# First FFN's weight sums on VectorE, and the output product's first blocks in the memory of a later step's sums

## The chip, the cores and the metric

The kernel is one program on one core of a Trainium2 chip. The core has five engines that run their own instruction streams in order: TensorE (PE in the profile, with PEld for its weight loads), VectorE (DVE), ScalarE (ACT), GpSimd (POOL) and SyncE (SP), which here does nothing but issue transfers. Work on one engine waits for another engine or for a transfer by semaphores. Tiles lie in SBUF; the products are accumulated in PSUM banks. Time is device time of one execution, in microseconds (us); the figure for a kernel is the median of its runs, and lower is better.

## What is computed

One layer of a decoder with 16 meta tokens in front of 1024 tokens, width 1024, all in float32:

```python
h = h + 0.5 * swiglu(rms_norm(h, ffn1_norm), ffn1_w_in, ffn1_w_out)   # first FFN
u = rms_norm(h, mix_norm) @ w_in
o = concat(hgrn2(u...), stick_breaking(u...))                         # the mixer
h = h + o @ w_out
h = h + 0.5 * swiglu(rms_norm(h, ffn2_norm), ffn2_w_in, ffn2_w_out)   # second FFN

def swiglu(h, w_in, w_out):
    g, u = split(h @ w_in, 2)          # w_in: 1024 x 5632, so g and u are 2816 wide
    return (silu(g) * u) @ w_out       # w_out: 2816 x 1024
```

The change lies in the two FFNs, in the first above all. An FFN has an *input product* (h @ w_in, then the gate silu(g) * u) and an *output product* (the gated activations @ w_out).

## The kernel before, in words

**Products.** A float32 product is made as three matmuls on a rounded type: each operand is split into a high half (a cast on ScalarE) and a low half (the operand minus its high half, on VectorE), and TensorE multiplies high by high, low by high and high by low. Both products of an FFN save an eighth of the multiplications with a scheme of Strassen and Winograd: operands are cut into 2 x 2 blocks, and seven products of sums of blocks stand for eight products of blocks.

**The input product** is `fast_in` (L351). It goes through the 2816 columns of g and u in eleven pairs of blocks of 128; of each pair of blocks it does first the gate's part and then the up part. Such a part is a *quad* (L450). A quad takes the four 128x512 blocks of w_in that belong to 256 columns and both halves of the depth: a11, a21, a22, a12. `block` (L368) has SP load each into a tile `raw`; there are `in_bufs` of them in turn (10 in the first FFN). Four sums are made of them, by `made` (L377; the instruction is L382, its tile is `s`): s1 = a21 + a22, s2 = s1 - a11, s3 = a11 - a21, s4 = a12 - s2. In this kernel they are made on GpSimd. `operand` splits a block or a sum into `wh` (ScalarE, L361) and `wl` (VectorE, L363). `times` (L441; its matmuls are L445) multiplies it in twelve matmuls of 512 columns by one of the seven operands of activations. The order of the seven products on TensorE, with the bank of PSUM each adds to, is

```
B11 (a11, qa)  T2 (s2, qb)  B21 (a12, qa)  T3 (s3, qb)  T1 (s1, qc)  T4 (a22, qb)  B22 (s4, qc)
```

Where two products go to one bank, the second adds to what the first left. Before that, partial sums that other outputs need are read out: `first` (L464) copies p1 from qa, and `kept` (L472; VectorE, L477) makes u2 = p1 + qb ahead of T3's product and u3 = p1 + qb after it. Then `take` hands each finished output on: for a gate quad to `gate` (VectorE L523, ScalarE's silu), for an up quad to `up` (VectorE L533 and L534), which multiplies by the gate. The up quad's outputs are four tiles `sg`; three are stored at once (L537). Of all four, `combined` (L543) makes the operands T1 to T4 of the output product by four subtractions on VectorE (L552 twice, L559, L562) and stores them through GpSimd's queue. In the first FFN `combined` is *put off*: it is appended to `put_off` and called in the next gate quad, behind the call that makes u3.

**Side work in the first FFN.** Meant to fill idle time of other engines, it is dealt out over the input product by hooks (`taken`, L1777): parts of other weights are read, split and stored to DRAM for later (`split_ahead`, L142; L152 loads, L179 and L180 split into a tile `both`, L174 stores it as `w2in` or `wout`), and x is turned (`turn_x`, L984). The meta tokens' input product (`meta_in`, L932) is made in small matmuls in the up quad; for it the gate's and the up's raw blocks are both held.

**The opening.** The first four pairs of quads of the first FFN (two in the second) are *opened*: they run interleaved while their activation operands are still made. In the first FFN `open_tokens` (L765) writes out the order by hand, as items 2 to 15. At item 4 it calls `prepare(0)` (L406), which loads the four blocks of the first quad and makes their four sums.

**The output product** is `fast_out` (L606). It goes through seven steps, each over eleven blocks q of 256 rows of w_out:

```
A12  A11  S1  S2  S4  S3  A22
```

`left(step, q)` (L644) gives the block or sum of w_out: S1 = A21 + A22, S2 = S1 - A11, S4 = A12 - S2, S3 = A11 - A21. Blocks that are needed once come into the ring of tiles `raw` (7 in the first FFN, 6 in the second); two tiles stay for the whole product: `sk`, eleven blocks that S1 fills first and S2 and S3 overwrite, and `ak`, eleven blocks of A11. `right` loads the activations, `halved` (L634) splits both into the tile `parts`, which has four places for weights, and the matmuls are L707. The meta tokens' output product (`meta`, L1875; `meta_block`, its matmuls are L1865) uses the raw blocks of A12, S3 and A22 and so holds them: in A12 it runs after every third q.

**What sets the order.** TensorE's order is written by hand. The other engines' orders come from a planner that goes by estimated costs and times at which operands are ready, except in the opening, where ScalarE's, VectorE's and SP's are by hand too. `self.tc.issue_after(x)` asks for no wait: it only puts what is issued under it behind x in the order of the same engine. `self.apart` is true in the first FFN's output product alone. The pools for the output product are laid over memory that the input product has used, and waits between old and new tiles are put in by the framework (`reuse_waits="tile"`, L49).

## Time and profile before

| | |
|---|---|
| median of 3 runs | 2025.84 us (2024.75 to 2028.49) |
| the profiled execution | 2025.31 us, its span 2023.6 us |
| mean granted clock of TensorE | 0.998 |
| first FFN, input product / output product | about 16 to 493 us / 493 to 722 us |
| second FFN, input product / output product | about 1376 to 1801 us / 1801 to 2014 us |

How to read the rows. A group of instructions is named by its line, its engine and its tiles, out<-in by the names in the program, with partitions x elements and how many there were; then the busy time in us with the mean of one in ns, and behind a second bar the idle time of the engine just before these instructions and what ended it ("<-DVE u L477": VectorE's instruction on `u` at line 477). A wait is read as "who waits, on which tile and line <- for whom: us in all, how many times, the longest". A time line's row has the start, the duration, the engine and the instruction. TensorE's clock is the clock that was granted, as a share of full speed.

### The profile page before, as it was taken

Reading aid. Unit: us, or ns where it says so; the run is one execution under the profiler, and the core shown is the slowest. Engines: PE = TensorE matmul, PEld = TensorE weight load, DVE = VectorE, ACT = ScalarE, POOL = GpSimd, SP = SyncE. Lnnn points to the kernel's source line nnn. Section 1 sums busy time; section 2 is a strip of 40 time slices with the busy share of each in tenths; the row PEclk is TensorE's granted clock in tenths of the full one; section 3 lists DMA queues with packets and bytes.
Section 4 is the critical chain, followed back from the end, with each engine's and each line's share of the span. In section 5 each row is a group of like instructions: output and inputs, shape, how many; then the busy total and the mean of one; then the engine's idle time right before and its main releaser. Section 6 shows DMA issues by size and latency. Waiting matters only on the chain.

```text
span 2023.6 us, 30784 instructions
## 1 busy us (share of the span) xinstructions
PE 1964.1 (97%) x10940; PEld 1647.1 (81%) x10940; DVE 1365.5 (67%) x2052; ACT 861.0 (43%) x1731; POOL 584.2 (29%) x692
## 2 busy tenths in 40 slices
PE   7999999999999999999999999999999999999998
PEld 6788787777778888897988888787888888888887
DVE  7877677787587663337777668548466776767774
ACT  6423343334344444356666644434132333244443
POOL 4344333332000002334333341320445544530000
PEclk9999999999999999999999999999999999999999
DMA  7257787656995406443545156674633332369463
GB/s 210 80 149 207 216 266 221 219 203 252 322 302 154 147 33 206 133 167 100 152 121 144 57 209 194 162 249 152 202 104 100 109 104 94 107 244 312 125 200 135
DMA packets 315577, 347.17 MB, mean 172 GB/s; under 512 B 61520, under 2 KB 216656, under 8 KB 315424
## 3 DMA queue, kind: packets, MB, share of 16 engines
q1 hardware_dynamic: 297136, 292.18, 46.5%
q0 software_dynamic: 17248, 53.03, 7.6%
q8 instruction: 86, 1.41, 0.3%
q14 instruction: 67, 0.55, 0.1%
q10 hardware_dynamic: 1040, 0.00, 0.0%
HBM read 233.75 MB, written 111.38 MB: 171 GB/s over the span
## 4 chain that ended last, share of the span: by engine, by line
PE 76%; DVE 4%; DMA 3%; issue 2%; ACT 1%; POOL 0%; SPq 0%; DVEq 0%; POOLq 0%; ACTq 0%
PE o L707 18%; PE qb L445 13%; PE qc L445 9%; PE qa L445 8%; PE proj L250 5%; PE proj L252 5%; PE proj L251 5%; PE flip L1398 2%; DMA raw<-in_ffn_w_out_dram 1%; PE wo L250 1%; PE wo L251 1%; PE wo L252 1%; PE lvl L1191 1%; PE oacc L1468 1%; PE oacc L1470 1%
## 5 line engine op out<-in xcount | busy, mean ns | idle before, releaser
L445 PE MATMUL qb<-T,wh 128*128 128x512 f32 x1056 | 348.2, 394 | 13.8 <-DVE u L477 11.8
L445 PEld LDWEIGHTS qb<-T,wh 128*128 128x128 f32 x1056 | 199.6, 189 | 62.9 <-issue 12.3
L445 PE MATMUL qa<-B,wh 128*128 128x512 f32 x696 | 227.5, 391 | 2.0 <-ACT both L469 1.7
L363 DVE TENSOR_TENSOR wl<-s,wh 128x512 fp32r<-128x512 f32 x160 | 184.2, 1151 | 57.1 <-ACT wh L361 55.8
L707 PE MATMUL o<-t,w 128*128 128x512 f32 x924 | 214.5, 391 | 4.1 <-DVE w L639 2.1
L250 PE MATMUL proj<-xh,wh 128*128 128x512 f32 (+2 forms) x640 | 216.5, 338 | 0.8 <-DVE st L1091 0.7
L252 PE MATMUL proj<-xl,wh 128*128 128x512 f32 (+2 forms) x640 | 209.7, 328 | 0.8 <-DVE xl L1853 0.8
L707 PE MATMUL o<-parts 128*128 128x512 f32 x924 | 209.9, 389 | 0.0
L251 PE MATMUL proj<-xh,wl 128*128 128x512 f32 (+2 forms) x640 | 209.8, 328 | 0.0
L445 PE MATMUL qb<-T,wl 128*128 128x512 f32 x528 | 206.9, 392 | 1.2 <-DVE wl L363 1.2
L707 PEld LDWEIGHTS o<-t,w 128*128 128x128 f32 x924 | 172.3, 188 | 43.6 <-DVE w L639 4.1
L707 PEld LDWEIGHTS o<-parts 128*128 128x128 f32 x924 | 173.4, 188 | 35.9
L361 ACT CAST wh<-s 128x512 fp32r<-128x512 f32 x160 | 99.4, 622 | 224.7 <-PE qb L445 181.0
L445 PEld LDWEIGHTS qa<-B,wh 128*128 128x128 f32 x696 | 130.5, 188 | 30.8 <-ACT both L469 1.9
L382 POOL TENSOR_TENSOR s<-raw 128x512 f32<-128x512 f32 x80 | 112.2, 1403 | 142.7 <-DMA raw<-in_ffn_w_in_dram 84.3
L361 ACT CAST wh<-raw 128x512 fp32r<-128x512 f32 x120 | 74.5, 622 | 148.1 <-PE qc L445 100.8
L445 PE MATMUL qa<-B,wl 128*128 128x512 f32 x348 | 135.5, 389 | 0.0
L252 PEld LDWEIGHTS proj<-xl,wh 128*128 128x128 f32 x640 | 120.5, 188 | 12.2 <-DVE xl L1853 1.2
L250 PEld LDWEIGHTS proj<-xh,wh 128*128 128x128 f32 x640 | 120.7, 189 | 11.4 <-DVE st L1091 1.2
L251 PEld LDWEIGHTS proj<-xh,wl 128*128 128x128 f32 x640 | 120.6, 188 | 9.1
L1550 POOL TENSOR_TENSOR sig<-sig,keep 128x144 f32<-128x144 f32 (+3 forms) x64 | 81.4, 1273 | 133.9 <-DVE keep L1544 79.9
L445 PEld LDWEIGHTS qb<-T,wl 128*128 128x128 f32 x528 | 99.9, 189 | 21.7 <-DVE wl L363 1.6
(392 smaller groups left out, 4042.5 us busy)
## 6 DMA issues: line engine op xcount, KB each, us to landing
raw<-in_ffn_w_in_dram SPq DMA_DIRECT2D x176, 256.0 KB, 4.0
raw<-in_ffn_w_out_dram SPq DMA_DIRECT2D x121, 256.0 KB, 4.5
w2in<-both SPq DMA_DIRECT2D x28, 512.0 KB, 3.2
raw<-in_w_in_dram SPq DMA_DIRECT2D x25, 512.0 KB, 4.1
ks<-kD SPq DMA_DIRECT2D x32, 260.0 KB, 4.7
wout<-both SPq DMA_DIRECT2D x16, 512.0 KB, 3.3
wh<-w2in SPq DMA_DIRECT2D x27, 256.0 KB, 3.3
wl<-w2in SPq DMA_DIRECT2D x27, 256.0 KB, 3.1
```

Source lines behind the costliest of these rows:

```text
L250: nc.tensor.matmul(ps, wh[:, s], xs, start=k == 0, stop=False)
L251: nc.tensor.matmul(ps, wl[:, s], xs, start=False, stop=False)
L252: nc.tensor.matmul(ps, wh[:, s], xl[:, k, c0 : c0 + n], start=False, stop=k == nk - 1)
L361: nc.scalar.copy(hi, src)
L363: nc.vector.tensor_sub(lo, src, hi.bitcast(F32))
L382: taken(op(t, x, y), False)
L445: nc.tensor.matmul(ps, a[:, k, :], b[:, k, :], start=start and k == 0 and i == 0, stop=k == 3 and i == 2, skip_group_check=True,)
L707: nc.tensor.matmul(banks[bank][m], y[:, m * P : (m + 1) * P], z, start=start and at == 0 and e == 0, stop=q == nq - 1 and e == 2, skip_gro ...
L1191: nc.tensor.matmul(ps[:, :, c, :], kp[:, P * c : P * c + P], strided(QA, P * c + n, (512 - n, 2), (2 * n, nb), (1, n)), start=True, stop=True,
L1398: self.nc.tensor.transpose(ps[:m, j, :], src[:, s0 : s0 + m], self.ident)
L1468: nc.tensor.matmul(o[:, c], vj, w[0], start=j == 0, stop=False, skip_group_check=True)
L1550: nc.gpsimd.tensor_mul(sig, sig, keep[:, 1 : nk + 1])
```

## The change

It has five parts.

1. In the first FFN the sums s1 to s4 of a quad are made on VectorE (`on`); those of `prepare(0)` stay on GpSimd, and so do the second FFN's.
2. `kept` remembers its last instruction, and the put-off `combined` is issued behind it: its four subtractions come behind u3 in VectorE's order.
3. In both FFNs the output product's first step, A12, loads its blocks into `sk[:, q]` and not into the ring. In the first FFN the meta tokens' matmuls for A12 are all made at the step's last q.
4. In the first FFN's output product what `left` issues on VectorE comes, in VectorE's order, behind the low half of the weights of four blocks before (`los[-4]`).
5. `prepare(0)` is called at item 11 of the opening and no longer at item 4.

```diff
--- before.py
+++ after.py
@@ -363,7 +363,7 @@
             nc.vector.tensor_sub(lo, src, hi.bitcast(F32))
             return hi, lo
 
-        loaded, put_off = [], []
+        loaded, put_off, last_kept = [], [], []
 
         def block(i, h, col):
             t = wp.tile([P, 4, P], F32, tag="raw", name="raw", bufs=self.in_bufs)
@@ -398,15 +398,17 @@
         prepared = {}
         quarters = (0, 0), (1, 0), (1, 1), (0, 1)
 
-        def first_sums(blocks, turns):
+        on = nc.vector if meta else nc.gpsimd
+
+        def first_sums(blocks, turns, on):
             a11, a21, a22, _ = blocks
-            s1 = made(a21, nc.gpsimd.tensor_add, a22, turns)
-            return s1, made(s1, nc.gpsimd.tensor_sub, a11, turns)
+            s1 = made(a21, on.tensor_add, a22, turns)
+            return s1, made(s1, on.tensor_sub, a11, turns)
 
         def prepare(col):
             blocks = [block(i, h, col) for i, h in quarters]
             a11, a21, _, a12 = blocks
-            s1, s2 = first_sums(blocks, 2)
+            s1, s2 = first_sums(blocks, 2, nc.gpsimd)
             s3 = made(a11, nc.gpsimd.tensor_sub, a21, 2)
             prepared[col] = blocks, (s1, s2, s3, made(a12, nc.gpsimd.tensor_sub, s2, 2))
 
@@ -427,16 +429,16 @@
             if sums:
                 s1, s2, s3, s4 = sums
             else:
-                s1, s2 = first_sums(blocks, turns)
+                s1, s2 = first_sums(blocks, turns, on)
             yield operand(s2)
             if not opened:
                 yield operand(a12)
-            yield operand(s3 if sums else made(a11, nc.gpsimd.tensor_sub, a21, turns))
+            yield operand(s3 if sums else made(a11, on.tensor_sub, a21, turns))
             if meta:
                 meta(col, [(q, b) for q, b in zip(quarters, blocks)])
             yield operand(s1)
             yield operand(a22)
-            yield operand(s4 if sums else made(a12, nc.gpsimd.tensor_sub, s2, turns))
+            yield operand(s4 if sums else made(a12, on.tensor_sub, s2, turns))
 
         def times(ps, w, x, start):
             (wh, wl), (xh, xl) = w, x
@@ -474,7 +476,9 @@
                     t = wp.tile([P, n], F32, tag="s", name=name, bufs=3)
                 else:
                     t = ev["p"].tile([P, n], F32, tag=name, name=name, bufs=1 if feed else 2)
-                taken(nc.vector.tensor_add(t, y, x), False)
+                last_kept[:] = [nc.vector.tensor_add(t, y, x)]
+                taken(last_kept[0], False)
+                last_kept[0] = last_kept[0].ins
                 return t
 
             if opened:
@@ -496,7 +500,8 @@
                 take(0, 0, go("a", "B21", False), None)
             u3 = kept("u3", p1, go("b", "T3", False))
             if put_off:
-                put_off.pop()()
+                with self.tc.issue_after(last_kept[0]):
+                    put_off.pop()()
             yield
             take(1, 1, go("c", "T1", True), u3)
             yield
@@ -636,10 +641,12 @@
             turns[name] = (i + 2) % 8
             hi, lo = (self.parts[name][:, j, :m] for j in (i, i + 1))
             nc.scalar.copy(hi, src)
-            nc.vector.tensor_sub(lo, src, hi.bitcast(F32))
+            at = nc.vector.tensor_sub(lo, src, hi.bitcast(F32))
+            if name == "w":
+                los.append(at.ins)
             return hi, lo
 
-        sub = nc.vector.tensor_sub
+        sub, los = nc.vector.tensor_sub, []
 
         def left(step, q):
 
@@ -665,9 +672,11 @@
                     return u, {(0, 0): a, (1, 0): s}
                 sub(a, a, raw(1, 0, q))
                 return a, {}
-            at = (0, 1) if step == "A12" else (1, 1)
-            t = raw(*at, q)
-            return t, {at: t}
+            if step == "A12":
+                nc.sync.dma_start(s, block(0, 1, q))
+                return s, {(0, 1): s}
+            t = raw(1, 1, q)
+            return t, {(1, 1): t}
 
         banks = {}
         delayed, opening = [], []
@@ -693,7 +702,8 @@
                     pout.tile([P, n], F32, tag=f"{bank}{m}", name="o") for m in range(4)
                 ]
             for q in range(nq):
-                src, blocks = left(a, q)
+                with self.tc.issue_after(los[-4]) if self.apart and len(los) > 4 else ExitStack():
+                    src, blocks = left(a, q)
                 act = right((q, b), n)
                 with self.tc.high_priority() if self.apart and a == "A12" and q < 3 else ExitStack():
                     wh, wl = halved(src, "w", 512)
@@ -892,13 +902,14 @@
         items = {
             2: lambda: (spare(2, 3), sums(1)),
             3: lambda: (spare(6, 7), sums(2)),
-            4: lambda: (self.row_sum(meta, 8, junk, nc.scalar), sums(3), prepare(0)),
+            4: lambda: (self.row_sum(meta, 8, junk, nc.scalar), sums(3)),
             5: roots,
             6: lambda: (spare(4, 5), scales()),
             7: lambda: (keep_b22(), nc.vector.tensor_copy(self.masks, sd)),
         }
         items.update({12 + j: lambda j=j: second(j) for j in range(4)})
-        items.update({8 + j: lambda j=j: combine(j) for j in range(4)})
+        items.update({8 + j: lambda j=j: combine(j) for j in range(3)})
+        items[11] = lambda: (prepare(0), combine(3))
         after = {6: turn_b22, 7: turn_b12, 8: turn_meta}
         for i in range(2, len(order)):
             if i + 2 < len(order):
@@ -1877,7 +1888,7 @@
                         if step not in banks_at:
                             return
                         held.extend((i, j, q, t) for (i, j), t in blocks.items())
-                        if q < last_q and (step == "S3" or q % 3 < 2):
+                        if q < last_q and (step != "A22" or q % 3 < 2):
                             return
                         for i, j, at, t in sorted(held, key=lambda x: x[0]):
                             new = at == 0 and i in banks_at[step]
```

## The prediction

> **What bounds the kernel now.** I read the page first, then the stretches of the span stage by stage, then who waited for whom on TensorE, then time lines around the longest waits.
>
> ```profile
> span 2023.6 us, 30784 instructions
> PE 1964.1 (97%) x10940; PEld 1647.1 (81%) x10940; DVE 1365.5 (67%) x2052; ACT 861.0 (43%) x1731; POOL 584.2 (29%) x692
> ```
>
> TensorE is busy for 97% of the span, so a change that adds no matmul and removes none can give back only stops of TensorE: 59.5 us in all. The stretches say where they lie (columns: the stretch and its length, then busy us per engine, the granted clock, the DMA share and GB/s).
>
> ```profile
> 325.00:350.00 25.00, 22.63 (x94) 18.24 (x93) 18.17 (x25) 9.89 (x17) 8.67 (x9) 0.93 0.58 186
> 450.00:475.00 25.00, 22.81 (x94) 18.45 (x94) 19.65 (x27) 11.10 (x20) 8.66 (x9) 0.93 0.50 184
> 62.00:100.00 38.00, 34.06 (x201) 26.69 (x200) 34.27 (x53) 18.76 (x36) 11.71 (x10) 1.00 0.25 77
> 240.00:480.00 240.00, 229.24 (x1276) 188.20 (x1275) 182.44 (x244) 91.61 (x164) 86.84 (x83) 0.99 0.68 221
> 493.00:580.00 87.00, 83.11 (x429) 65.39 (x430) 58.22 (x97) 32.02 (x58) 4.88 (x9) 1.00 0.97 334
> ```
>
> The change touches three places that stop: the opening (62 to 100: 3.9 us idle, VectorE 90% busy), the later pairs of the first FFN's input product (240 to 480: 10.8 us idle, and two slices at clock 0.93), and the start of its output product (493 to 580: 3.9 us idle, DMA share 0.97). The longest of TensorE's waits from 240 to 480 (us in total, times, longest):
>
> ```profile
> PE qb L445 <- DVE u L477: 10.0, 6, 2.4
> ```
>
> All but 0.8 us of the idle time from 240 to 480 is a wait for `u` (L477), the partial sum that VectorE must read out of bank qb before T3's product may add to it. This is VectorE, then GpSimd, then TensorE at one such wait:
>
> ```profile
> 323.03 0.68 DVE L552 TENSOR_TENSOR t<-sg 128x512 f32<-128x512 f32 x1
> 323.75 0.69 DVE L552 TENSOR_TENSOR t<-sg,t 128x512 f32<-128x512 f32 x1
> ...
> 324.96 0.69 DVE L559 TENSOR_TENSOR sg<-sg 128x512 f32<-128x512 f32 x1
> 325.56 1.75 DVE L562 TENSOR_TENSOR sg<-sg,t 128x512 f32<-128x512 f32 x1
> 327.24 0.68 DVE L477 TENSOR_TENSOR u<-qb,p 128x512 f32<-128x512 f32 x1
> ...
> 325.29 1.47 POOL L382 TENSOR_TENSOR s<-raw,s 128x512 f32<-128x512 f32 x1
> ...
> 328.06 4.58 PE qb L445 x12
> 332.63 2.73 PE qc L445 x12
> ```
>
> The bank was full at about 322.9, but `u` stood behind the four subtractions of `combined` (L552, L552, L559, L562), the last of them stretched to 1.75 us beside a GpSimd sum. The wait costs 2.4 us, and then twelve matmuls take 4.58 us where the next twelve take 2.73.
>
> **The change, part by part.**
>
> *`combined` is put behind `u3`* (the `issue_after` at L499). The four subtractions leave the place ahead of `u2`: the 10.0 us go, and with them the slow clock of two slices, 2 x 25 x 0.07 = 3.5 us. Late next is gate (1,1) at L523: it must read qc before B22's product adds to it, T4's product or 2.7 us after T1 ends; four subtractions at 0.6 us started after `u3` end 2.4 us after T3, before T1 is through. The stores of T1 to T4 go later as well, and gate (1,0) rewrites the tile that T4's store reads: VectorE may stand there for 2 to 3 us, with no weight behind it that TensorE needs sooner. I take 13.0 of the 13.5 us; bounds 0 (the third rival) and 13.5.
>
> *The sums go from GpSimd to VectorE.* Groups from 240 to 480, mean ns of one after the busy us:
>
> ```profile
> L363 DVE TENSOR_TENSOR wl<-s,wh 128x512 fp32r<-128x512 f32 x46 | 40.8, 887 | 10.1 <-ACT wh L361 9.7
> L363 DVE TENSOR_TENSOR wl<-raw,wh 128x512 fp32r<-128x512 f32 x33 | 27.2, 823 | 0.2
> L477 DVE TENSOR_TENSOR u<-qb,p 128x512 f32<-128x512 f32 x23 | 15.8, 686 | 8.4 <-PE qb L445 8.4
> L534 DVE TENSOR_TENSOR sg<-u,sg 128x512 f32<-128x512 f32 x15 | 15.7, 1046 | 0.0
> L562 DVE TENSOR_TENSOR sg<-sg,t 128x512 f32<-128x512 f32 x6 | 8.4, 1402 | 0.0
> L382 POOL TENSOR_TENSOR s<-raw 128x512 f32<-128x512 f32 x22 | 32.8, 1492 | 46.7 <-DMA raw<-in_ffn_w_in_dram 20.5 <-DVE wl L363 13.6 <-ACT wh L361 6.5
> L382 POOL TENSOR_TENSOR s<-raw,s 128x512 f32<-128x512 f32 x12 | 16.7, 1390 | 57.2 <-DVE wl L363 57.1
> ```
>
> VectorE's instructions of this size take 0.69 us where one input is PSUM (L477), and these four groups on SBUF alone 0.82 to 1.40. Their excess over 0.69 is 9.2 + 4.5 + 5.4 + 4.3 = 23.4 us and would go; the sums come back at 0.69: 22 and 12 of the two rows and as many of s2 as of s4, 46, or 32 us. So VectorE's load stays as it is, within 9 us of 240, at 76%: no gain and no loss on the path, as long as it has room. The Trainium skill, "Perfetto Trace Analysis", Optimizing Scalar/DVE Operations, warns that moving work between GpSimd and VectorE might not help, since they share a read port; these groups bear it out. By that rule the opening, next, would give nothing either, and the sum would be 0.8 us higher.
>
> *`prepare(0)` goes from item 4 to item 11.* Its four loads pass seven single blocks in SP's queue and its four sums stay on GpSimd, later; the next quad's four sums join VectorE between 55 and 88. The 3.9 us idle from 62 to 100 are waits for VectorE. Four sums cost 2.8 us there, and GpSimd's stretching of its neighbours goes: I take a gain of 0.8 us, bounds 3.9 gained and 2.8 lost.
>
> *A12's blocks lie in `sk`, and VectorE's sums there stay four blocks behind.* The ring holds seven blocks, and meta's matmuls keep three at a time. TensorE's 493.31 to 580 and the stops in it:
>
> ```profile
> L707 PE MATMUL o<-t,w 128*128 128x512 f32 x341 | 80.8, 394 | 4.1 <-DVE w L639 2.1 <-ACT w L638 1.3 <-DVE u L533 0.5
> L1865 PE MATMUL m<-raw,actm 128*32 128x128 f32 x88 | 3.2, 277 | 0.0
> 515.99 0.49 PE L707 MATMUL o<-t,w 128*128 128x512 f32 x1 [1.30 <-ACT w L638]
> 564.02 0.69 DVE L658 TENSOR_TENSOR raw<-raw,sk 128x512 f32<-128x512 f32 x1 [2.29 <-DMA raw<-in_ffn_w_out_dram]
> ```
>
> 341 matmuls at 2.73/12 = 0.2275 us are 77.6 us, 88 small ones 3.2 at most, of 86.7: 5.9 us or more are stops and their slow restarts. The one at 516 waits for a block that the ring had no place for; the one at 566 has VectorE standing for a load of S4, two steps ahead. Both causes go: a gain of 5.9 us, bounds 3.9 (the idle time alone) and 6.9. Grouping A12's meta matmuls at its end is counted at nothing: they are as many as before.
>
> *But `sk` is memory that the input product still uses.* The ring's `raw` lies where B11 and B21 were, which are free long before the end. In the program of before `sk` lies over `p1`, `sg00`, `both` and `sum`, and the first write to a new tile waits for all tiles under it: the first load of `ak` waits for GpSimd's last sum, whose tiles are under another part of `ak`. So A12's first load will wait until the last store from `both` has landed. First FFN, before: the end of the input product, the output product's start, the last two stores of `both`, ScalarE's casts (a row of the page), three halves of A12's weights on VectorE; then median us from issue to landing at 492 to 512 (two rows) and at 474 to 480:
>
> ```profile
> 492.29 0.53 PE L948 MATMUL mf<-pick,mt 128*128 128x32 f32 x4
> 493.31 1.86 PE L707 MATMUL o<-t,w 128*128 128x512 f32 x7 [0.49 <-DVE u L533]
> 495.59 1.52 SPq L174 DMA_DIRECT2D w2in<-both  x2
> L361 ACT CAST wh<-s 128x512 fp32r<-128x512 f32 x160 | 99.4, 622 | 224.7 <-PE qb L445 181.0
> 487.66 1.89 DVE L639 TENSOR_TENSOR w<-raw,w 128x512 fp32r<-128x512 f32 x3
> w2in<-both SPq DMA_DIRECT2D x3, 512.0 KB, 5.0
> raw<-in_ffn_w_out_dram SPq DMA_DIRECT2D x3, 256.0 KB, 5.0
> raw<-in_ffn_w_out_dram SPq DMA_DIRECT2D x2, 256.0 KB, 3.0
> ```
>
> The last store is issued at 496.8; without the three halves ahead of it, which now wait too, at 494.9. It lands 5.0 us later, A12's load 5.0 after that, ScalarE's cast takes 0.6: TensorE starts at 505.5 instead of 493.31, and slowly (4.58 - 2.73 = 1.8 us more). Cost 14.0 us. Bounds: with 3.0 us for both transfers TensorE starts at 501.5, 8.2 late, no slow start; at 496.8 and with 7.1 us for the load (next fence) 16.2 + 1.8 = 18.0. SP's queue stands behind that load, but what lies there (A11's loads) has 30 us.
>
> *The same in the second FFN*, where `sk` lies over T1 and T4. Before: B22's product begins, which is T4's end, and the output product begins; then landing times at 1796 to 1806:
>
> ```profile
> 1797.88 0.39 PE L445 MATMUL qc<-B,wh 128*128 128x512 f32 x1
> 1800.60 1.07 PE L707 MATMUL o<-parts 128*128 128x512 f32 x4
> raw<-in_ffn_w_out_dram SPq DMA_DIRECT2D x4, 256.0 KB, 7.1
> ```
>
> The load can go at 1797.9; with 5.0 us and 0.6 for the cast TensorE starts at 1803.5, 2.9 us late, and half of the stops of about that length (two of four at 325 to 460) were followed by a slow start: 0.9 more, 3.8. Bounds 0.9 (3.0 us for the load) and 6.8 (7.1, and 1.8). The Trainium skill, "TensorE: Matmul & The Clock Gate", What's actually happening, has the clock fall only after an idle window of about 3.4 us; by that rule this stop would cost 2.9 and the sum be 0.9 us lower. The 0.93 slice after a 2.4 us wait speaks against it.
>
> The sum against the profiled execution, which took 2025.31 us beside its span of 2023.6 (median of the runs 2025.84): 2025.3 - 13.0 - 0.8 - 5.9 + 14.0 + 3.8 = 2023.4.
>
> **The rivals.**
>
> *Faster: the new waits are short.* If the transfers around both ends take 3.0 us, they cost 8.2 + 0.9 and not 17.8: 2023.4 - 8.7 = 2014.7. For it: the DMA queues were nearly free at 474 to 480. Against: share 0.97 from 493 on.
>
> *Slower: VectorE, which takes its queue in order, stands at the sums for weight blocks that are late.* GpSimd stood for such loads 20.5 us from 240 to 480, in three waits (longest 7.6). VectorE has one spare stretch per pair, 3.7 us before `u` (L533: 18.3 us in five), and T1's bank allows another 2.7 us. Up to 6.4 us a wait costs nothing; at 7.6 it costs 1.2 us in each of nine pairs, 10.8, and their slow restarts more, so that about the 13.0 us gained are lost: 2036.4.
>
> ```profile
> POOL s L382 <- DMA raw<-in_ffn_w_in_dram: 20.5, 3, 7.6
> L533 DVE TENSOR_TENSOR u<-qc,u 128x512 f32<-128x512 f32 x10 | 6.8, 682 | 18.3 <-PE qc L445 18.3
> ```
>
> *The change doesn't do what it says*, since `sk` would be free early: then the two waits cost nothing, 2005.6. The wait of `ak` speaks against it; I give it 0.03.
>
> **How the numbers follow.** Against no change a measurement tells about 0.2%, 4 us. The forecast, gains and new waits that nearly cancel, has 0.40, with a range of its own from 2017 to 2030: of it 0.11 fall under 2021.8, 0.23 within, 0.06 above 2029.9. Short waits 0.27 and the early `sk` 0.03, all faster; VectorE standing 0.30, slower. Faster 0.41, same 0.23, slower 0.36. The range for 8 in 10 reaches from within the short waits to just past VectorE standing: 2009 to 2038.
>
> **What would show it.** No wait of qb for L477 from 240 to 480 shows the first step; L562 near 0.69 us the second. The window 493 to 580 should hold one stop of about 12 us at its start, TensorE waiting for ScalarE's cast of `sk` and that for a load, and no other; 1800.6 a stop of about 3 us. If the stops at the two seams are absent, my reading of `sk` is wrong; if VectorE's list of waits names loads of in_ffn_w_in, the slower rival holds.

## The result, and the profile after

The changed kernel takes 2029.13 us (median of 15 runs, 2025.92 to 2033.40), the kernel before 2025.84 (15 runs, 2022.89 to 2030.70): a ratio of 1.0013 with a 95% interval from 1.0004 to 1.0023. It is slower, by about 0.13%, less than the 0.2% that the prediction called no change. The forecast was 2023.4, so the time lies inside the range given, but on the other side of the kernel before. The profiled executions, 2028.28 against 2025.31 us, differ by 3.0 us, and the stages below account for them.

In the changed kernel the line numbers are shifted: the input product's matmuls are L447, u2 and u3 L479, `up` L538, the four subtractions of `combined` L557, L564 and L567, the output product's matmuls L717, its splits L643 and L644, the meta tokens' L1876. First TensorE's waits in the first FFN and, by a second question, from 1790 to 1830 (us in all, times, longest):

```profile
PE o L717 <- ACT w L643: 14.1, 1, 14.1
PE xps L770 <- DVE row L761: 13.4, 3, 11.4
PE qc L447 <- DVE u L538: 2.2, 3, 1.0
PE qb L447 <- DVE u L479: 1.3, 1, 1.3
...
PE o L717 <- ACT parts L643: 6.4, 1, 6.4
```

The waits of qb for the partial sum, 11.8 us in eight before, are down to one, in the opening. Two new waits stand in their place, one at the start of each output product: TensorE waits for ScalarE's cast of A12's first block. The stretches that answer to those shown of before (stretch, length, busy us of PE, PEld, DVE, ACT and POOL, granted clock, DMA share, GB/s):

```profile
62.00:100.00 38.00, 35.56 (x209) 28.37 (x208) 35.53 (x63) 19.44 (x35) 1.17 (x3) 1.00 0.25 77
240.00:480.00 240.00, 236.12 (x1383) 195.60 (x1381) 186.27 (x303) 95.72 (x175) 22.71 (x42) 1.00 0.73 238
493.00:580.00 87.00, 87.00 (x456) 71.88 (x455) 54.06 (x87) 36.13 (x64) 2.16 (x4) 0.99 0.91 310
492.44:495.59 3.15, 3.15 (x8) 2.48 (x8) 2.62 (x4) 1.82 (x3) 0.00 (x0) 0.50 1.06 395
1800.45:1806.16 5.71, 5.71 (x14) 4.46 (x14) 4.95 (x6) 1.86 (x3) 2.67 (x4) 0.50 1.04 409
```

In the opening's stretch TensorE idles for 2.4 us, 1.5 less than before, and from 240 to 480 for 3.9 us and not 10.8, although the end of that stretch already lies in the new stop. The last two rows are the matmuls just behind the two stops: a granted clock of 0.50 for 3.15 and for 5.71 us, so half of each is lost, 1.6 and 2.9 us.

Stage by stage, in us, from the starts of the first and the last matmul of each product (the last plus 0.23):

| | before | changed | difference |
|---|---|---|---|
| first FFN, input product ends | 492.3 | 477.8 | -14.5 |
| from there to the output product's first matmul | 1.0 | 14.6 | +13.6 |
| output product's length | 229.2 | 224.0 | -5.2, of it +1.6 at half clock |
| mixer | 653.2 | 652.7 | -0.5 |
| second FFN, input product's length | 424.8 | 424.7 | -0.1 |
| from there to the output product's first matmul | 0.0 | 6.6 | +6.6 |
| output product's length | 213.4 | 216.3 | +2.9, all at half clock |
| the rest | | | +0.2 |
| sum | | | +3.0 |

VectorE's groups from 240 to 478 show the second step of the prediction:

```profile
L363 DVE TENSOR_TENSOR wl<-s,wh 128x512 fp32r<-128x512 f32 x45 | 30.8, 685 | 6.3 <-ACT wh L361 6.2
...
L382 DVE TENSOR_TENSOR s<-raw 128x512 f32<-128x512 f32 x21 | 14.5, 689 | 20.2 <-DMA raw<-in_ffn_w_in_dram 20.1
L539 DVE TENSOR_TENSOR sg<-u,sg 128x512 f32<-128x512 f32 x17 | 11.7, 688 | 0.0
...
L567 DVE TENSOR_TENSOR sg<-sg,t 128x512 f32<-128x512 f32 x6 | 4.1, 686 | 0.0
```

Each of these takes 0.69 us now, where the same ones (L363, L534 and L562 of before) took 0.82 to 1.40 on the mean beside GpSimd's sums, and the sums cost 0.69 each: from 240 to 480 VectorE's load is 186.3 us where it was 182.4.

### The profile page after: what moved, and what is told of

Its sections match the earlier page's. It is cut to its first block, busy times and chain, and to the rows that moved or that the text cites. A ratio compares the mean times of both kernels' runs of the same rounds, so it can differ in the third digit from the quotient of the medians.

```text
span 2026.3 us, 30704 instructions
## 1 busy us (share of the span) xinstructions
PE 1960.7 (97%) x10940; PEld 1650.1 (81%) x10940; DVE 1364.6 (67%) x2136; ACT 860.6 (42%) x1731; POOL 462.6 (23%) x608
## 4 chain that ended last, share of the span: by engine, by line
PE 90%; DVE 4%; DMA 3%; ACT 1%; issue 1%; SPq 0%; DVEq 0%; ACTq 0%
PE o L717 21%; PE qb L447 17%; PE qa L447 12%; PE qc L447 11%; PE proj L250 5%; PE proj L252 5%; PE proj L251 5%; PE flip L1409 2%; PE wo L250 1%; PE wo L251 1%; PE wo L252 1%; PE lvl L1202 1%; PE oacc L1479 1%; PE oacc L1481 1%; PE mq L981 1%; PE z L1545 1%
## 5 line engine op out<-in xcount | busy, mean ns | idle before, releaser
L447 PE MATMUL qb<-T,wh 128*128 128x512 f32 x1056 | 345.0, 391 | 2.6 <-DVE u L479 1.3
L447 PEld LDWEIGHTS qb<-T,wh 128*128 128x128 f32 x1056 | 198.2, 188 | 47.8 <-issue 2.5
L447 PE MATMUL qa<-B,wh 128*128 128x512 f32 x696 | 226.9, 391 | 0.3 <-ACT B L820 0.2
L717 PE MATMUL o<-t,w 128*128 128x512 f32 x924 | 213.0, 392 | 14.1 <-ACT w L643 14.1
L717 PE MATMUL o<-parts 128*128 128x512 f32 x924 | 212.8, 393 | 6.4 <-ACT parts L643 6.4
L717 PEld LDWEIGHTS o<-t,w 128*128 128x128 f32 x924 | 174.1, 189 | 51.0 <-ACT w L643 14.2
L717 PEld LDWEIGHTS o<-parts 128*128 128x128 f32 x924 | 175.4, 190 | 43.4 <-ACT parts L643 6.8
L447 PE MATMUL qb<-T,wl 128*128 128x512 f32 x528 | 205.9, 390 | 1.2 <-DVE wl L363 1.2
L363 DVE TENSOR_TENSOR wl<-s,wh 128x512 fp32r<-128x512 f32 x160 | 165.8, 1036 | 50.2 <-ACT wh L361 49.2
L447 PEld LDWEIGHTS qa<-B,wh 128*128 128x128 f32 x696 | 130.6, 188 | 27.9 <-DVE B L821 0.5
L447 PE MATMUL qa<-B,wl 128*128 128x512 f32 x348 | 135.6, 390 | 0.0
L447 PE MATMUL qc<-B,wh 128*128 128x512 f32 x352 | 115.2, 391 | 2.2 <-DVE u L538 2.2
L447 PE MATMUL qc<-T,wh 128*128 128x512 f32 x352 | 117.2, 394 | 0.0
L447 PEld LDWEIGHTS qb<-T,wl 128*128 128x128 f32 x528 | 99.2, 188 | 21.6 <-DVE wl L363 1.6
```

Of the source, the lines that this page charges most:

```text
L363: nc.vector.tensor_sub(lo, src, hi.bitcast(F32))
L447: nc.tensor.matmul(ps, a[:, k, :], b[:, k, :], start=start and k == 0 and i == 0, stop=k == 3 and i == 2, skip_group_check=True,)
L717: nc.tensor.matmul(banks[bank][m], y[:, m * P : (m + 1) * P], z, start=start and at == 0 and e == 0, stop=q == nq - 1 and e == 2, skip_gro ...
```

## The experiments

Two questions stood against each other at each place. For the stops: do they come from `sk` lying on memory that is still in use, or from transfers that are slow there whatever memory they go to? For the gain: did the order behind u3 bring it, or the sums?

**A12 back in the ring, in both FFNs**, the rest of the change kept.

```diff
-            if step == "A12":
-                nc.sync.dma_start(s, block(0, 1, q))
-                return s, {(0, 1): s}
-            t = raw(1, 1, q)
-            return t, {(1, 1): t}
+            at = (0, 1) if step == "A12" else (1, 1)
+            t = raw(*at, q)
+            return t, {at: t}
...
-                        if q < last_q and (step != "A22" or q % 3 < 2):
+                        if q < last_q and (step == "S3" or q % 3 < 2):
```

> A12's blocks go back into the ring in both FFNs, with the meta tokens' matmuls of A12 after every third q as before; the other four parts of the change stay. Memory theory: both stops at the start of the output products come from sk lying over memory that the input product still uses. In the changed kernel they are 14.3 us and 1.6 us of half-speed matmuls behind it in the first FFN, 6.6 us and 2.6 us in the second: 25.1 us, of which the seams of before had 0.7. The stops inside A12 and S1 that the changed kernel lost (2.0 to 2.9 us) return. 2029.1 - 24.4 + 2.5 = 2007, range 2003 to 2012, faster than before by 0.7 to 1.1%. Rival, crowded queues: the first weights are late because transfers are slow there (5 to 7 us each), whatever memory they go to; then most of the stops stay, 2022 or more.

Measured: 2008.05 us, 0.9915 of before (0.9902 to 0.9928). Both stops are gone; what is left at the start of the first output product is small:

```profile
PE o L715 <- ACT w L643: 0.8, 1, 0.8
PE o L715 <- DVE u L538: 0.5, 1, 0.5
PE o L715 <- DVE w L644: 0.2, 1, 0.2
```

The first wait is the ring's, 22 us into A12. The first output product takes 225.4 us, against 224.0 - 1.6 = 222.4 with A12 in `sk`: as memory for A12, `sk` is worth 3.0 us there. (The four kernels below that keep A12 in `sk` there and start it with one stop take 222.3 to 222.4 us too, with the half clock taken off; the two other ring kernels take 226.2 and 226.4, so it is 3 to 4 us.) In the second FFN it is worth nothing: 213.4 us before, with A12 in the ring, and 216.3 - 2.9 = 213.4 in the changed kernel.

**A12 in the ring in the second FFN alone.**

```diff
-            if step == "A12":
+            if step == "A12" and self.apart:
                 nc.sync.dma_start(s, block(0, 1, q))
...
-            t = raw(1, 1, q)
-            return t, {(1, 1): t}
+            at = (0, 1) if step == "A12" else (1, 1)
+            t = raw(*at, q)
+            return t, {at: t}
```

> The changed kernel with A12 in the ring in the second FFN alone; the first FFN keeps A12 in sk. Memory theory: the stop of 6.6 us and the 2.6 us of slow matmuls at 1794 to 1806 go, 2029.1 - 9.2 = 2020 (2018 to 2022). What I predicted for this seam was 3.8 us: if that size were right for a median run, 2025.3. Crowded queues: 2027 to 2029.

Measured: 2021.78 us, 0.9981 of before (0.9972 to 0.9989), 7.4 us under the changed kernel. The profiled execution starts the second output product at once (1797.0) and takes 213.4 us over it, so that stop and half clock are gone whole. The table has 9.4 us for this seam, I had given it 3.8; the medians, 7.4 apart, bear out most of the 9.4.

**Without the order behind u3.**

```diff
-                with self.tc.issue_after(last_kept[0]):
-                    put_off.pop()()
+                put_off.pop()()
```

> The changed kernel without the order behind u3: the put-off subtractions are placed by the planner again, which puts them ahead of u2. If it is the place of the subtractions that gained, TensorE waits of qb for L479 come back in the later pairs, a little shorter than before since no GpSimd sum stretches L562: 4 or 5 waits of 1.3 to 2.4 us with a slow restart for the longer ones, 7 to 13 us: 2036 to 2042. Rival: moving the sums to VectorE is what gained; then 2028 to 2031.

Measured: 2030.74 us, 1.0024 of before (1.0014 to 1.0034): 1.6 us above the changed kernel, in the rival's range, and the two intervals overlap. There is no wait of qb for L479 from 240 to 478. The input product ends at 479.3, where seven profiles of kernels with the changed kernel's input product, its own among them, have it end at 476.9 to 480.9: taking the order away from the changed kernel costs nothing that shows. What that says of the order follows only from the next two together.

**The kernel before with the order alone.** The edit is part 2 of the change; GpSimd makes the sums.

```diff
...
-                taken(nc.vector.tensor_add(t, y, x), False)
+                last_kept[:] = [nc.vector.tensor_add(t, y, x)]
+                taken(last_kept[0], False)
+                last_kept[0] = last_kept[0].ins
...
-                put_off.pop()()
+                with self.tc.issue_after(last_kept[0]):
+                    put_off.pop()()
```

> The kernel before with one edit: the put-off subtractions are issued behind u3 on VectorE. If the place of the subtractions made the waits of qb for L477, these go and the input product of the first FFN ends 10 to 13 us sooner: 2013 (2011 to 2016). Rival, from the run without the order, which lost only 1.6 us: the waits came from a backlog of VectorE, whose instructions take up to 1.8 us beside GpSimd's sums; then the backlog stays and shows at other instructions (gate and up reading qb and qc, the weights' low halves), and the gain is half or less: 2018 to 2025.

Measured: 2008.84 us, 0.9921 of before (0.9907 to 0.9934), a larger gain than either theory gave. VectorE in the stretch shown of before:

```profile
321.44 0.68 DVE L477 TENSOR_TENSOR u<-qb,p 128x512 f32<-128x512 f32 x1
322.04 1.40 DVE L363 TENSOR_TENSOR wl<-s,wh 128x512 fp32r<-128x512 f32 x1
324.02 1.13 DVE L363 TENSOR_TENSOR wl<-raw,wh 128x512 fp32r<-128x512 f32 x1 [0.57 <-ACT wh L361]
325.60 0.69 DVE L477 TENSOR_TENSOR u<-qb,p 128x512 f32<-128x512 f32 x1 [0.45 <-PE qb L445]
326.20 0.68 DVE L555 TENSOR_TENSOR t<-sg 128x512 f32<-128x512 f32 x1
```

u2 goes as soon as VectorE reaches it, u3 waits for TensorE and not TensorE for it, and the subtractions follow. Instructions are still stretched beside GpSimd, to 1.40 here, and it does not matter: the input product ends at 476.8, 15.5 us sooner, and the output product behind it is 1.8 us shorter (227.5). The backlog that the rival spoke of exists but TensorE does not pay for it.

**The kernel before with the sums alone.**

```diff
+        on = nc.vector if meta else nc.gpsimd
...
-            s1 = made(a21, nc.gpsimd.tensor_add, a22, turns)
-            return s1, made(s1, nc.gpsimd.tensor_sub, a11, turns)
+            s1 = made(a21, on.tensor_add, a22, turns)
+            return s1, made(s1, on.tensor_sub, a11, turns)
```

(s3 and s4 in the same way, the prepared quad's stay on GpSimd.)

> The kernel before with one edit: the sums of the first FFN's weight blocks on VectorE, those of the prepared quad still on GpSimd. If the backlog beside GpSimd's sums made the waits, they go without any new order: the input product ends 10 to 14 us sooner, 2012 to 2016. If it was the place of the subtractions, as I predicted (sums worth nothing): 2024 to 2027.

Measured: 2009.28 us, 0.9917 of before (0.9905 to 0.9930), a larger gain than either theory gave. VectorE at the same place, then in the next pair, and there the first matmul behind T2's product and the first of T3's:

```profile
317.15 0.68 DVE L554 TENSOR_TENSOR t<-sg,t 128x512 f32<-128x512 f32 x1
317.75 0.68 DVE L479 TENSOR_TENSOR u<-qb,p 128x512 f32<-128x512 f32 x1
318.35 0.68 DVE L561 TENSOR_TENSOR sg<-sg 128x512 f32<-128x512 f32 x1
...
357.65 0.68 DVE L554 TENSOR_TENSOR t<-sg 128x512 f32<-128x512 f32 x1
...
360.18 0.68 DVE L564 TENSOR_TENSOR sg<-sg,t 128x512 f32<-128x512 f32 x1
360.78 0.68 DVE L479 TENSOR_TENSOR u<-qb,p 128x512 f32<-128x512 f32 x1
...
358.85 0.39 PE L447 MATMUL qa<-B,wh 128*128 128x512 f32 x1
361.61 0.47 PE L447 MATMUL qb<-T,wh 128*128 128x512 f32 x1
```

At 317 the planner puts u2 between the second and the third subtraction. That is not what cures the wait, though: in four of the six pairs from 235 to 445, the one at 357 among them, all four subtractions stand ahead of u2 as before, and TensorE doesn't wait. Two things differ there. The first subtraction starts 1.2 to 1.9 us ahead of the moment at which T2's product is done (357.65 against 358.85), where at the four long waits of before it started between 0.4 us ahead and 0.2 us behind it; and the last one takes 0.68 us and not 1.75 to 1.77. In the kernel before, the two pairs without a stretched subtraction (waits at 242 and 285) still cost 0.6 and 0.7 us, against 1.8 to 2.4 with one: the stretched one makes about 1.1 us of a long wait, VectorE's lateness the rest. u2 ends 0.15 us ahead of T3's first matmul at 361, so there is hardly any room left.

So the order and the sums are two cures of one wait, and each alone brings the whole of it: the input product ends at 476.8 with the first, 478.1 with the second, 477.8 with both, no further apart than profiles of the same input product. The wait needed both, four subtractions ahead of u2 and a VectorE that came to them late; the rival's backlog was half of the truth. What made VectorE earlier with the sums on it, fewer stretched instructions or another order ahead of the subtractions, was not tested.

**`sk` and `ak` swapped in the first FFN**, so that A12's memory comes free earlier.

```diff
-        sk = op.tile([P, nq, 512], F32, name="sk")
-        ak = op.tile([P, nq, 512], F32, name="ak")
+        at = [op.tile([P, nq, 512], F32, name=x) for x in (("ak", "sk") if self.apart else ("sk", "ak"))]
+        ak, sk = at if self.apart else at[::-1]
```

> The changed kernel with the two long tiles of the first FFN's output product laid in the other order: ak first and sk behind it, so that sk lies over the last sum and the old ring and no longer over both, sg00 and p1. Memory theory: A12's first load no longer waits for the last store from both (landed 486.8) but for the last reading of a sum (481.2 on VectorE), so that TensorE starts 5.7 us sooner, at 486.7 in place of 492.4; A11's loads into ak wait instead, with 30 us to spare. 2023.4 (2021.5 to 2025.5). Rival, crowded queues, or the release being something other than memory: 2028 to 2030.

Measured: 2028.65 us, 1.0016 of before (1.0007 to 1.0026), no better than the changed kernel. SP's queue in the changed kernel:

```profile
481.24 0.32 SPq L174 DMA_DIRECT2D w2in<-both  x1
481.61 1.95 SPq L1965 DMA_DIRECT2D hT<-xD  x2
483.66 1.15 SPq L634 DMA_DIRECT2D act<-act18B  x1
486.99 1.48 SPq L676 DMA_DIRECT2D sk<-in_ffn_w_out_dram  x3
```

and in the swapped one, then (KB, median us from issue to landing) the transfer issued at 483.99:

```profile
481.18 0.32 SPq L174 DMA_DIRECT2D w2in<-both  x1
481.55 1.86 SPq L1965 DMA_DIRECT2D hT<-xD  x2
483.51 0.44 SPq L634 DMA_DIRECT2D act<-act18B  x1
483.99 2.37 SPq L676 DMA_DIRECT2D sk<-in_ffn_w_out_dram  x2
```

```profile
sk<-in_ffn_w_out_dram SPq DMA_DIRECT2D x1, 256.0 KB, 7.8
```

The memory does come free earlier: the load goes at 483.99. In the changed kernel it went only at 486.99, when the last store from `both` had landed (issued 481.24, 5.6 us). But it takes 7.8 us to land where it took 4.8, and lands at 491.8 in both. Here the two theories are both right, one behind the other.

**The same, with the ring loads of S1 and the loads of hT behind A12's** in the first FFN. Each is put behind the last load of A12 that the program has made before it; for the four loads of hT within A12 that is one in between, and not the last of the eleven.

```diff
...
-            nc.sync.dma_start(t, block(i, j, q))
+            with self.tc.issue_after(self.a12[-1]) if self.a12 and self.apart else ExitStack():
+                nc.sync.dma_start(t, block(i, j, q))
...
-                nc.sync.dma_start(s, block(0, 1, q))
+                self.a12.append(nc.sync.dma_start(s, block(0, 1, q)).ins)
...
-                            nc.sync.dma_start(hT[:, m, c : c + n], xD[m, :, c : c + n])
+                            with tc.issue_after(self.a12[-1]):
+                                nc.sync.dma_start(hT[:, m, c : c + n], xD[m, :, c : c + n])
...
```

> The kernel with ak and sk swapped in the first FFN, and there too the ring loads of S1 and the loads of hT behind A12's. With the swap alone the first load was issued 3 us sooner (484.0) and landed no sooner (491.8). If the memory is one limit and the crowded queues the next, taking two hT loads out of the way lets it go at 481.6 and land at 486.6 to 489: TensorE starts at 487.3 to 489.7 in place of 492.5, which from the swap's 2028.7 gives 2023.5 to 2026. If the landing is set by the stores in flight alone (512 KB from both, T1 to T4), nothing: 2028 to 2029.

Measured: 2028.22 us, 1.0017 of before (1.0007 to 1.0026). TensorE does start sooner, and stops again:

```profile
487.73 2.08 PE L720 MATMUL o<-t,w 128*128 128x512 f32 x4 [10.28 <-ACT w L646]
491.17 31.30 PE L720 MATMUL o<-t,w 128*128 128x512 f32 x128 [1.36 <-ACT w L646]
522.40 2.61 PE L1879 MATMUL m<-sk,actm 128*32 128x128 f32 x88
```

The first block is issued at 480.75, ahead of all loads of hT, and lands at 487.0, 4.7 us sooner. The second, issued at 482.15 behind one load of hT, takes 8.3 us, and TensorE, back at half clock, stops for it. A12 ends at 522.4, that is 45.5 us after the input product's end, where the changed kernel needs 46.2. The first block alone was the limit no longer; the DMA share is 1.03 there, and loads of hT (481.25, 483.14, 485.91 and 490.49) still go between A12's. What A12's loads would do with every load of hT behind them was not tested.

**The second FFN's ring loads of S1 and loads of hT behind A12's.**

```diff
...
-            nc.sync.dma_start(t, block(i, j, q))
+            with self.tc.issue_after(self.a12[-1]) if self.a12 and not self.apart else ExitStack():
+                nc.sync.dma_start(t, block(i, j, q))
...
-                        nc.sync.dma_start(hT[:, m, c : c + n], self.h2D[m, :, c : c + n])
+                        with tc.issue_after(self.a12[-1]):
+                            nc.sync.dma_start(hT[:, m, c : c + n], self.h2D[m, :, c : c + n])
```

> The changed kernel; in the second FFN the ring loads of S1 and the loads of hT are put behind A12's loads in SP's queue. In the changed kernel three ring loads stand ahead of A12's first load, which is issued at 1792.6, 1.4 us after its memory came free, and takes 7.2 us to land. If the queue ahead is the size that I missed, the load goes at 1791.2 and lands in 5 us or a little more: TensorE starts 2.5 to 3.5 us sooner, 2026 (2024.5 to 2027), and less if the slow restart shrinks. If the size is set by the stores and activations in flight, not by these loads: 2028 to 2029.

Measured: 2025.48 us, 1.0003 of before (0.9994 to 1.0011), 3.6 us under the changed kernel, whose SP queue at that place, and then the landing time of its first A12 load, are:

```profile
1790.63 1.86 SPq L629 DMA_DIRECT2D raw<-in_ffn_w_out_dram  x4
1792.59 0.89 SPq L676 DMA_DIRECT2D sk<-in_ffn_w_out_dram  x1
```

```profile
sk<-in_ffn_w_out_dram SPq DMA_DIRECT2D x1, 256.0 KB, 7.2
```

In this kernel, in four views: the load in SP's queue, its landing time, the wait of TensorE and the stretch behind it.

```profile
1792.14 0.33 SPq L679 DMA_DIRECT2D sk<-in_ffn_w_out_dram  x1
```

```profile
sk<-in_ffn_w_out_dram SPq DMA_DIRECT2D x1, 256.0 KB, 5.3
```

```profile
PE o L720 <- ACT parts L646: 3.1, 1, 3.1
```

```profile
1798.18:1803.88 5.70, 5.70 (x13) 4.46 (x14) 4.05 (x4) 1.86 (x3) 4.53 (x5) 0.50 1.04 398
```

The load goes the moment T4's product ends, lands in 5.3 us, and the wait is 3.1 us, half of the 6.4. The half clock stays 5.7 us long. So of the seam's cost about 3.3 us were ring loads in front of A12's first (the first load of hT stood behind it in the changed kernel already), and 2.9 us are the restart, which a stop half as long can cost as well.

**The ring kernel without the bound on VectorE's runahead.**

```diff
-                with self.tc.issue_after(los[-4]) if self.apart and len(los) > 4 else ExitStack():
+                if True:
                     src, blocks = left(a, q)
```

> The changed kernel with A12 in the ring, less the bound on VectorE's runahead in the first FFN's output product. I predicted that bound and A12 in sk would give 5.9 us together; with A12 in the ring and the bound the product took 225.4 us, without either 227.5 to 229.2. If the bound is what removes the stop near S4's late load (2.1 us and a slow restart), the product takes 228 again: 2008.1 + 2.6 = 2010.7. Rival: the stop is gone because the sums and the order changed when VectorE arrives; then 225.4 stays and 2008.

Measured: 2010.48 us (four runs), 0.9928 of before (0.9913 to 0.9943), an interval that overlaps the ring kernel's. VectorE stands at S4's late load again, 2.0 us in one wait, but the product takes 226.2 us and not 228, against 225.4. What the bound is worth, 0.8 us in these two profiles, can't be told from nothing: the next kernel has the bound and takes 226.4.

**The ring kernel with the prepared quad at item 4 again.**

```diff
-            4: lambda: (self.row_sum(meta, 8, junk, nc.scalar), sums(3)),
+            4: lambda: (self.row_sum(meta, 8, junk, nc.scalar), sums(3), prepare(0)),
...
-        items[11] = lambda: (prepare(0), combine(3))
+        items[11] = lambda: combine(3)
```

> The changed kernel with A12 in the ring, and the prepared quad made at item 4 of the opening as before. Predicted for the move to item 11: a gain of 0.8 us (3.9 gained to 2.8 lost), so 2008.9 here and a stop of TensorE near 82 us that the other lacks (1.2 us in the run with the order alone). Rival: what shortened the opening is the next quad's sums on VectorE, not the move; then the stops from 60 to 100 stay as in the ring kernel, and 2008.

Measured: 2006.17 us (four runs), 0.9906 of before (0.9890 to 0.9923), the lowest median of all, though its interval overlaps those of the other kernels without the two stops. Its opening is as good as the changed kernel's, here and with the sums alone, and that with the order alone is as before. The row of this kernel, then of the sums alone:

```profile
62.00:100.00 38.00, 35.62 (x211) 28.13 (x210) 35.65 (x63) 19.85 (x37) 1.64 (x4) 1.00 0.27 83
```

```profile
62.00:100.00 38.00, 35.63 (x211) 28.16 (x210) 35.68 (x63) 20.08 (x37) 1.62 (x3) 1.00 0.27 83
```

With the order alone TensorE is busy for 34.2 us there, before 34.1. The opening's 1.5 us came from the sums; the move to item 11 brought nothing that shows. It may have cost something ahead of that stretch: from 0 to 62 TensorE is busy for 49.1 to 50.3 us in the four profiles with the quad at item 4, and for 46.9 to 49.0 in the eight with it at item 11. The medians don't settle it.

## Why the prediction was right or wrong

*`combined` behind u3, 13.0 us:* right. The input product, opening included, ends 14.5 us sooner, where 13.8 were predicted, and the order alone brings 15.5. The reading of the wait at 325 was right as far as it went: u2 stood behind four subtractions. But the four alone didn't make the wait, as the pairs of the sums alone show, and in the changed kernel the gain can't be put down to the order: taken away, it costs nothing that shows.

*The sums on VectorE, neutral:* right for the load (186.3 us against 182.4 from 240 to 480), and right in the sum by luck: the prediction saw the subtraction stretched to 1.75 us at the wait, yet gave its going no part in the cure. The sums alone cure the same wait, since VectorE comes to the subtractions sooner and none is stretched; that they add nothing is because the order had cured it already. The rule of the Trainium skill that was quoted ("Perfetto Trace Analysis", Optimizing Scalar/DVE Operations) agrees as far as VectorE's load goes, but the run with the sums alone, 16 us faster, shows that load is not all that such a move changes.

*The opening, 0.8 us:* 1.5 us by the stretch, from the sums, which were to cost 2.8 there, and not from the moved item.

*A12 in `sk` and the bound, 5.9 us:* 6.8 us without the half clock (229.2 to 224.0, and 1.6), inside its bounds of 3.9 to 6.9. `sk` is 3 to 4 of them by the ring kernels; the bound isn't shown to bring any, and without `sk` and bound the order alone already has 1.8 and the sums alone about 1 of them. Where the rest comes from stays open.

*The first FFN's seam, 14.0 us:* the mechanism stands, down to the engines: the last store from `both`, then the load, then ScalarE's cast. Transfers of 5.6 and 4.8 us for my 5.0 and 5.0; a stop 13.6 us longer, and 1.6 at half clock for my 1.8, make 15.2. What was not in it is the second limit: with the memory free 3 us sooner the load landed no sooner.

*The second FFN's seam, 3.8 us:* this is the term that failed; it measured 9.4 us (6.6 of stop, 2.9 at half clock, rounded), above the bound of 6.8. Three sizes were wrong, all in one direction. I let the load go when T4's product ended; 1.4 us of ring loads for S1 now stood ahead of it in SP's queue, since A12 no longer used the ring and its places were free. I had looked past SP's queue at the seam of the first FFN, but not at what the emptied ring would let through here. I took 5.0 us for the landing and kept 7.1 as a bound; 7.2 came. And I gave the restart half a chance, 0.9 us, from stops inside the input product, where 2.9 were lost; of the three this one is the least certain, since behind like stops of 6.2 and 6.3 us at this seam (the swapped kernel and the one with its loads first) the half clock lasted 4.9 and 3.1 us and not 5.7. With 9.4 in its place the sum is 2023.4 + 5.6 = 2029.0; the other terms are off by 1.2 us or less and nearly cancel.

*The rivals.* VectorE does stand at late weight loads, as the slower rival has it: 20.1 us in five waits from 240 to 478. But the longest is 4.7 us, and three stops of TensorE at L538, 2.2 us together, are the whole price. The allowance of 6.4 us was too kind: waits of 4.3 and 4.7 us cost 0.7 and 1.0.

*The chances.* 0.41 on faster leaned on the lower cases of both seams, transfers of 3 us, for which only the quiet time ahead of them spoke. Both came out at the middle or above it.

## What to carry to other kernels

A tile that is loaded first in a stage should not lie on memory that the stage before still uses: one seam here cost 15 us and the other 9, and between them they ate a change whose other steps gave 21 (14.5 and 6.8). Loads through buffers that are free early (the ring here) had no such stop. Letting the first load go 3 and 6 us sooner (483.99 and 480.75 against 486.99) did not bring the time back. When a step gives up its buffers, ask which later loads will take them, since these then stand in the same queue ahead of what is urgent.

Where one engine's order is planned, a wait that looks like one misplaced instruction can go by two edits; try each alone before adding them up, and look at every place of the wait, not at one, before saying how an edit cured it. Here either alone, on the kernel before, gives 2009 us, and no kernel with more of the parts was faster beyond the intervals.

## What the runs showed of the hardware

The granted clock behind a stop at the start of an output product is 0.50 to 0.52 for 3.1 to 6.5 us, where no second stop cuts that short, and that length doesn't follow the stop's: 3.15 us after one of 14.1, 5.71 after one of 6.4, 5.70 after one of 3.1. At one and the same place, the start of the first output product, it was 3.15, 3.99, 4.35, 4.37 and 6.07 us in five kernels with stops of 13.5 to 14.2 us. The first row is the longest of these, from the kernel without the order; the kernel before shows slow matmuls after 2.4 us as well (TensorE's wait ends at 328.06; the third row is the wait), and after one of its two waits of 2.2 us (ending at 458.29, the fourth row) but not after the other (415.28, the last):

```profile
493.66:499.73 6.07, 6.07 (x15) 4.78 (x15) 2.60 (x4) 1.84 (x3) 0.00 (x0) 0.51 1.04 391
328.06:331.74 3.68, 3.68 (x9) 2.86 (x10) 2.58 (x2) 0.00 (x0) 2.97 (x3) 0.55 1.13 318
325.31:328.06 2.75, 0.38 (x2) 0.03 (x1) 2.75 (x4) 1.10 (x2) 2.40 (x3) 1.00 1.09 395
458.29:461.41 3.12, 3.12 (x8) 2.44 (x8) 2.56 (x2) 0.00 (x0) 2.41 (x3) 0.50 0.53 213
415.28:418.40 3.12, 3.12 (x14) 2.60 (x15) 2.70 (x3) 0.05 (x1) 2.41 (x3) 1.00 0.61 236
```

Each stop with slow matmuls behind it thus costs 1.5 to 3.3 us again, half of the slow stretch, and what decides its length, or whether it comes at all, is open. The Trainium skill, "TensorE: Matmul & The Clock Gate", What's actually happening, has the clock fall after an idle window of about 3.4 us and rise after a busy one as long; the slow rows after 2.2, 2.4 and 3.1 us do not agree with the first, nor those of 5.7 and 6.07 us with the second. The same page says that the window runs freely, so that the slow stretch differs from run to run; the five lengths at one place agree with that, though no run here shows the window itself.

In the crowded stretch at 480 to 500 a 256 KB load that is issued 3 us sooner lands at the same time, 491.8, and takes 7.8 us in place of 4.8. With the loads of hT no longer ahead of it, issued at 480.75, it took 6.3 us and landed at 487.0. Both fit a landing time that goes by what is already in flight, which no run here separates from the rest.
